# Stationary values in three kinds of attention, and one branch for an expert's gate and up products

## The chip, the cores and the metric

One kernel runs as one program on one core of a Trainium2 chip. The metric is the device time of one execution in microseconds (us), the median of several. Engines: TensorE (PE, matrix products; PEld is its weight load), VectorE (DVE), ScalarE (ACT), GpSimd (POOL) and SyncE (SP), which here issues the loads. Data lies in HBM, on chip in SBUF, and products land in PSUM.

## The reference

256 positions of width 1024 go through two blocks of two layers each, all in float32.

```python
# first block, layers i = 0 and 1: 16 query heads, 4 key/value heads, of 64
q, k, v = project_qkv(x, w_qkv[i], cos, sin)
a = moba_attention(q, k, v) if i == 0 else sliding_window_attention(q, k, v, sinks[0])
x = layer_norm(alpha * x + a @ w_o[i], ...)
f = swiglu(x, ...) if i == 0 else moe_swiglu(x, ...)
x = layer_norm(alpha * x + f, ...)
x = x + (p[i] @ w_ple_proj[i]) * sigmoid(x @ w_ple_gate[i])
...
# sliding window, with one sink per head
e = exp(logits - m)
probs = e / (sum(e) + exp(sink - m))
...
# eight experts, the best two of each position; expert: (silu(x Wg) * (x Wu)) Wd, width 3584
top_v, top_i = top_k(logits, 2)
# second block, both layers: gated delta rule (4 heads of 128) beside dilated attention
# (8 heads of 64, three dilations merged by their denominators), then a convolved GLU of 2816
```

With 256 positions the first layer's attention is plain causal attention, and one causal softmax with a table of weights does the three dilations.

## The kernel before

The Python code lists all operations of the network in program order. A planner (class Plan) then chooses, operation by operation, what each engine does next, by estimated costs and by how much work still hangs on an operation, and writes out one fixed order for each engine; a change in one place therefore reorders the neighbourhood. Nearly every instruction is issued by `call` (L756; copies by ACT at L754), so lines tell little, and tiles are known by tags: `raw` (5 slots of 512 KB for weights), `w4` (8), `v4` (4), `kv` (2), `mx` (15, in the experts only, where hi, lo and r4 give up their room by `layout(1)`), and in PSUM A (2), B (4) and C (2). Where the planner expects PE to idle, it may put in filler products (`identb`, 128x512, bf16).

Float32 weights outside the experts are split into a rounded part `hi` (ACT) and a rest `lo` (DVE or POOL), with three products each (A<-hi,r and so on).

Attention: `first_layer` calls `att_pair` for two parts (8 heads each) and two blocks b of 128 positions, four calls a layer; a dilated attention (in `mixer`) calls it for b = 0 and 1. With nk = b + 1 key blocks, scores of two groups of four heads land in PSUM C and B, DVE takes the row maximum, ACT the exponential (P). `att_out` then transposes P on PE, copies it out, multiplies it with V, which has a column of ones as its 65th so that the denominator comes out with the product (P as stationary operand, V moving, L1183), and DVE divides. `part_T` transposes the result (four 128x128) and splits it for the output projection w_o. Between the parts, `dense_tok` makes the query products of the next part, and the first half of w_o's contraction is done beside the second part.

Experts: `route` gives each position its slot among an expert's first 96. `fetch` loads the first 22 weight units (128x1024 float32) before the way into the experts. There, PE reads the eight counts into registers (L751), and all engines pass a branch over code for an expert with more than 96 rows (`overflow_experts`, L1634 and L294; jumped over with this input). Then, expert by expert, `expert_up` and `expert_out` go through four chunks of the width (1024, 1024, 1024, 512); a full chunk is 8 units of gate, 8 of up and 8 of down, 672 units in all. `tiled` multiplies slots 0 to 63 with each unit (stationary 64 columns, two halves of a unit side by side), and then, under a branch (L733) on the count over 64, slots 64 to 95 (stationary 32, four quarters side by side). A unit's slot comes free after both. With this input experts 1, 3, 6 and 7 take these branches. `raw_moe` is the rota by which units take their slots (28, of tags m = mx, r = raw, w = w4, v = v4, k = kv). `gather_pair` makes one-hot matrices of two experts on DVE and gathers their rows on PE.

Of the kernel before, what the change touches and what calls it, by code (L numbers as in the profile page):

```python
# [11 lines left out]
F32 = mybir.dt.float32  # L12
# [221 lines left out]
class Plan:  # L234
# [511 lines left out]
    def call(self, op, method, args, kw):  # L746
# [37 lines left out]
class Net:  # L784
    def __init__(self, ctx, tc, a, out):
# [8 lines left out]
        self.ahead = []  # L794
# [186 lines left out]
    def load(self, w, k0, nk, c0, n, tag=None):  # L981
# [4 lines left out]
        for h in range(2):  # L986
            raw = nc.tile([128, m, n], F32, "raw", *(tag or self.next_raw()))
            r0 = k0 + 128 * m * h
            nc.sync.dma_start(raw, lambda r0=r0: w[span(r0, 128 * m), span(c0, n)].rearrange("(t p) c -> p t c", p=128))
            raws.append(raw)  # L990
# [127 lines left out]
    def values(self, b, acc, n, va):  # L1118
        self.copy_out(va[:, b, :, 0:64], acc.rearrange("p (h d) -> p h d", d=64))

    def att_pair(self, kind, qT, kT, va, b, p, a):
# [6 lines left out]
        for g in (2 * p, 2 * p + 1):  # L1128
# [5 lines left out]
            groups.append((g, heads, self.ta([128, 4, nk, 128], "P"), self.sm([128, 4], "nm")))  # L1134
        for i0 in range(0, 4, per):
# [9 lines left out]
            with nc.group():  # L1145
                for i in range(per):
                    for kb in range(nk):
                        for ps, (_, heads, _, _) in zip(pss, groups):
# [5 lines left out]
            for ps, (g, heads, P, nm) in zip(pss, groups):  # L1154
# [9 lines left out]
    def att_out(self, kind, va, b, g, heads, P, nm, a):  # L1164
        nc = self.nc
        grouped = kind != "dilated"
        nk = b + 1
        per = 4 // nk
        PT = self.ta([128, 4, nk, 128], "PT")
        for i0 in range(0, 4, per):  # L1170
            ps = (self.pb if grouped else self.pa)([128, per, nk, 128], "PTp")
# [4 lines left out]
        po = (self.pb if grouped else self.pa)([128, 4, 65], "po")  # L1176
        for i in range(4):
            for kb in range(nk):
                nc.tensor.matmul(po[:, i, :], lhsT=PT[:, i, kb, :], rhs=va[:, kb, heads[i][3], :],
                                 start=kb == 0, stop=kb == nk - 1)  # L1180
        den = self.sm([128, 4, 1], "den")
        if kind == "swa":
            es = self.sm([128, 4], "es")  # L1183
            nc.vector.tensor_tensor(out=es, in0=nm, in1=self.nsink[:, 4 * g:4 * g + 4], op=OP.subtract)
            nc.scalar.activation(es, es, AF.Exp)
            nc.vector.tensor_tensor(out=den, in0=po[:, :, 64:65], in1=es[:, :, None], op=OP.add)
            nc.vector.reciprocal(den, den)
        else:
            nc.vector.reciprocal(den, po[:, :, 64:65])
        if grouped:  # L1190
            o = a[:, (g % 2) * 256:(g % 2) * 256 + 256].rearrange("p (h d) -> p h d", d=64)
        else:
            o = a.rearrange("p (i s d) -> p i s d", s=2, d=64)[:, :, g, :]
        nc.vector.tensor_tensor(out=o, in0=po[:, :, 0:64], in1=den.to_broadcast([128, 4, 64]), op=OP.mult)
# [233 lines left out]
    def gather_pair(self, e, xs, pos):  # L1428
# [736 lines left out]
```

## Time and profile before

| | us |
|---|---|
| median of 3 runs | 2221.87 |
| lowest and highest | 2221.15, 2225.56 |
| the profiled execution | 2224.77 |
| its span | 2223.0 |
| PE busy | 2102.1 |
| DVE, ACT, POOL busy | 984.3, 751.7, 224.7 |

Stages, in us from the span's start: first attention some 45 to 87, its output projection and norm to 125, FFN to about 390, second attention about 400 to 465, its output projection, norm and router to 492, experts to 1419, combine, norm and gate to 1478, the second block's layers to about 1850 and 2223, with dilated attention around 1600 to 1640 and 1960 to 2000.

How to read rows: a timeline row has the start, the length of a run of like instructions, engine, line, operation, what it writes from what, shapes and a count, and in brackets how long the engine idled before it and on whom. A matrix product's shape has the stationary operand's rows*columns first. Consecutive products overlap, so one that is counted costs the distance of starts. A stretches row has the stretch, its length, the busy time of PE, PEld, DVE, ACT and POOL (with counts), PE's granted clock, the mean busy share of 16 DMA engines, and GB/s. The trace has two records for each float32 product of the program.

### The profile page before, as it was taken

How to read it: one execution, taken by the hardware profiler on the slowest of the kernel's cores; microseconds unless marked ns; L12 is line 12 of the kernel's file. 1: busy time of each engine (PE TensorE's matmuls, PEld its weight loads, DVE VectorE, ACT ScalarE, POOL GpSimd, SP SyncE). 2: the span in 40 equal slices, each digit the busy share in tenths (PEclk: the TensorE clock that was granted, in tenths of full speed). 3: DMA queues.
4: the chain of work that ended last, by engine and by line, in shares of the span. 5: the costliest groups of instructions: out<-in, count | busy, mean ns of one | idle time of the engine just before them, and what ended most of it. 6: DMA issues, size and time to landing. Idle time of an engine off the chain costs nothing. (4 is left out here: it accounts for less than half of the span.)

```text
span 2223.0 us, 35510 instructions
## 1 busy us (share of the span) xinstructions
PE 2102.1 (95%) x14582; PEld 1449.2 (65%) x14582; DVE 984.3 (44%) x1670; ACT 751.7 (34%) x1141; POOL 224.7 (10%) x147
## 2 busy tenths in 40 slices
PE   8999999988799989998979999899999999999998
PEld 6899997763334323433233434479979997988997
DVE  6665467651010101010101001467687768768666
ACT  5544444420011101110110000356465556456554
POOL 0110001120000000000000000218020005411000
PEclk9999999989899999999999999999999999999999
DMA  7356664349999999999999998544455664435563
GB/s 251 111 165 192 184 184 152 114 159 345 404 388 370 373 404 409 385 372 404 408 404 394 369 396 326 188 145 144 130 170 183 190 183 141 124 97 187 175 194 117
DMA packets 246476, 557.48 MB, mean 251 GB/s; under 512 B 21320, under 2 KB 108552, under 8 KB 246280
## 3 DMA queue, kind: packets, MB, share of 16 engines
q1 hardware_dynamic: 246280, 554.72, 69.9%
q8 instruction: 141, 2.31, 0.4%
q14 instruction: 55, 0.45, 0.1%
HBM read 553.60 MB, written 1.05 MB: 250 GB/s over the span
## 5 line engine op out<-in xcount | busy, mean ns | idle before, releaser
L756 DVE TENSOR_TENSOR lo<-raw,hi 128x1024 fp32r<-128x1024 f32 x324 | 404.7, 1257 | 200.3 <-PE B L756 94.6
L756 ACT ACTIVATE hi<-raw 128x1024 fp32r<-128x1024 f32 x364 | 382.2, 1062 | 292.8 <-PE B L756 123.5
L756 PE MATMUL B<-r,hi 128*128 128x256 f32 x2112 | 388.2, 282 | 0.0
L756 PEld LDWEIGHTS B<-r,hi 128*128 128x128 f32 x2112 | 342.0, 191 | 17.7
L756 PE MATMUL B<-mx,w 128*64 128x512 f32 (+3 forms) x2188 | 327.9, 458 | 10.6 <-DMA mx<-in_w_exp_up_dram 8.4
L756 PE MATMUL A<-hi,r 128*128 128x512 f32 x896 | 334.3, 410 | 0.9 <-DVE v L756 0.6
L756 PE MATMUL B<-r,lo 128*128 128x256 f32 x1056 | 298.6, 283 | 0.0
L756 PEld LDWEIGHTS B<-mx,w 128*32 128x32 f32 (+1 forms) x2188 | 111.0, 124 | 153.1 <-issue 104.3
L756 PEld LDWEIGHTS B<-r,lo 128*128 128x128 f32 x1056 | 201.5, 191 | 0.0
L756 PEld LDWEIGHTS A<-hi,r 128*128 128x128 f32 x896 | 171.1, 191 | 32.2 <-DVE v L756 1.4
L756 PE MATMUL C<-hi,r 128*128 128x512 f32 x512 | 185.1, 400 | 1.1 <-ACT kv L756 1.1
L756 DVE MEMSET B<- 128x256 f32 (+1 forms) x64 | 15.7, 245 | 370.0 <-ACT w L756 366.6
L756 PE MATMUL A<-lo,r 128*128 128x512 f32 x448 | 177.4, 396 | 0.2 <-DVE lo L756 0.2
L756 PE MATMUL B<-w,w 128*128 128x128 f32 (+4 forms) x1252 | 168.4, 363 | 0.3 <-PEq L733 0.3
L756 PE MATMUL A<-mx,v 128*32 128x256 f32 (+1 forms) x960 | 162.1, 491 | 0.2 <-PEq L733 0.2
L754 ACT ACTIVATE v<-C 128x512 f32<-128x512 f32 (+2 forms) x63 | 29.4, 467 | 379.8 <-PE C L756 336.0
L756 DVE TENSOR_TENSOR w<-w,B 128x256 f32<-128x256 f32 (+2 forms) x79 | 41.8, 529 | 247.9 <-PE B L756 229.7
L756 POOL TENSOR_TENSOR lo<-raw,hi 128x1024 fp32r<-128x1024 f32 x40 | 102.0, 2563 | 487.8 <-ACT hi L756 367.4
L756 PEld LDWEIGHTS B<-w,w 128*128 128x128 f32 (+2 forms) x1252 | 104.5, 155 | 51.4 <-issue 39.6
L756 ACT ACTIVATE w<-B 128x256 f32<-128x256 f32 (+3 forms) x95 | 44.7, 475 | 264.8 <-PE B L756 242.9
L756 PEld LDWEIGHTS C<-hi,r 128*128 128x128 f32 x512 | 98.5, 192 | 18.8 <-ACT kv L756 1.9
L756 PE MATMUL B<-raw,w 128*64 128x512 f32 (+3 forms) x648 | 100.9, 463 | 1.3 <-DMA raw<-in_w_exp_up_dram 1.0
(239 smaller groups left out, 2602.1 us busy)
## 6 DMA issues: line engine op xcount, KB each, us to landing
mx<-in_w_exp_up_dram SPq DMA_DIRECT2D x124, 512.0 KB, 10.2
mx<-in_w_exp_down_dram SPq DMA_DIRECT2D x120, 512.0 KB, 10.3
mx<-in_w_exp_gate_dram SPq DMA_DIRECT2D x119, 512.0 KB, 8.0
raw<-in_ffn_up_dram SPq DMA_DIRECT2D x88, 512.0 KB, 3.7
raw<-in_w_in_dram SPq DMA_DIRECT2D x56, 512.0 KB, 3.8
raw<-in_w_exp_down_dram SPq DMA_DIRECT2D x48, 512.0 KB, 10.2
w<-in_w_exp_up_dram SPq DMA_DIRECT2D x46, 512.0 KB, 10.2
raw<-in_ffn_down_dram SPq DMA_DIRECT2D x44, 512.0 KB, 4.5
```

Source lines behind the costliest of these rows:

```text
L754: eng.activation(args[0], args[1], AF.Copy)
L756: getattr(eng, method)(*args, **kw)
```

## The change

- `att_pair` now sums each exponential (`accum_out`), adds the sink's term in the sliding window, takes the reciprocal and multiplies P by it, before P is transposed (`heads_last`). `att_values` multiplies with V stationary (64 columns, no ones) and the transposed P moving, two groups side by side, so that the result comes out already transposed and goes straight to the split. `att_out` and `part_T` behind it are gone.
- w_o is loaded by heads (`by_heads`), each load as two of 64 partitions.
- `fetch` takes 28 units; the first 7 (raw and kv slots) before `layout(1)`. The steady rota has 24 slots: no v, no k.
- `tiled` takes gate and up together: both 64-slot passes, then one branch with both 32-slot passes.
- `values_load` is made without its bounds check. The first pair's one-hots are made ahead of the overflow branch.

```diff
-            kw["to"].cell[0] = self.nc.values_load(args[0], engines=[mybir.EngineType.PE], min_val=0, max_val=S)
+            kw["to"].cell[0] = self.nc.values_load(args[0], engines=[mybir.EngineType.PE],
+                                                       skip_runtime_bounds_check_because="it is the sum of 256 zeros and ones")
...
-        self.raw_first = [("raw", RAW)] * RAW + [("kv", 2)] * 2 + [("mx", 15)] * 15
-        size = {"m": ("mx", 15), "r": ("raw", RAW), "w": ("w4", 8), "v": ("v4", 4), "k": ("kv", 2)}
-        self.raw_moe = [size[c] for c in "mrmwmrmvmwmkmrmwmrmvmwmkmrmm"]
+        self.raw_first = [("raw", RAW)] * RAW + [("kv", 2)] * 2 + [("mx", 15)] * 15 + [("w4", 8)] * 4 + [("v4", 4)] * 2
+        size = {"m": ("mx", 15), "r": ("raw", RAW), "w": ("w4", 8)}
+        self.raw_moe = [size[c] for c in "mrmwmmrmwmmrmwmmrmwmmrmm"]
...
+            if self.by_heads:
+
+                for s in range(2):
+                    r0 = k0 + 256 * s + 64 * m * h
+                    nc.sync.dma_start(raw[64 * s:64 * s + 64], w[r0:r0 + 64 * m, c0:c0 + n].rearrange("(t p) c -> p t c", p=64))
...
-        va = self.nc.tile([128, 2, HK, 65], F32, "va", "kv", 2)
-        self.nc.gpsimd.memset(va, 1.0)
+        va = self.nc.tile([128, 2, HK, 64], F32, "va", "kv", 2)
...
-                for i in range(per):
-                    nc.scalar.activation(P[:, i0 + i], ps[:, i], AF.Exp, bias=nm[:, i0 + i:i0 + i + 1])
-        for g, heads, P, nm in groups:
-            self.att_out(kind, va, b, g, heads, P, nm, a)
...
+                hs = slice(i0, i0 + per)
+                for i in range(i0, i0 + per):
+                    nc.scalar.activation(P[:, i], ps[:, i - i0], AF.Exp, bias=nm[:, i:i + 1], accum_out=den[:, i])
+                if kind == "swa":
+                    es = self.sm([128, per, 1], "es")
+                    nc.vector.tensor_tensor(out=es[:, :, 0], in0=ns, in1=self.nsink[:, 4 * g + i0:4 * g + i0 + per], op=OP.subtract)
+                    nc.scalar.activation(es, es, AF.Exp)
+                    nc.vector.tensor_tensor(out=den[:, hs], in0=den[:, hs], in1=es, op=OP.add)
+                nc.vector.reciprocal(den[:, hs], den[:, hs])
+                part = P[:, hs].rearrange("p i k j -> p i (k j)")
+                nc.vector.tensor_tensor(out=part, in0=part, in1=den[:, hs].to_broadcast([128, per, nk * 128]), op=OP.mult)
+        self.att_values(kind, va, b, [(heads, P) for _, heads, P, _, _ in groups], [t[k] for t in aT.tiles])
...
+        PT = [self.heads_last(P, nk, pool) for _, P in groups]
+        po = pool([128, 4, 128], "po")
+        with nc.group():
+            for i in range(1 if grouped else 4):
+                hs = slice(None) if grouped else i
+                for kb in range(nk):
+                    for s, (heads, _) in enumerate(groups):
+                        nc.tensor.matmul(po[64 * s:64 * s + 64, hs], lhsT=va[:, kb, heads[i][3], :], rhs=PT[s][:, hs, kb, :],
+                                         start=kb == 0, stop=kb == nk - 1)
+        self.split_ps(po, *[t[:, :, b * 128:b * 128 + 128] for t in dst])
...
+        for acc, tiles in sums:
+            for k, u in enumerate(tiles):
+                n = u.shape[1]
+                with nc.group():
+                    for i in range(2):
+                        mm(acc[0][64 * i:64 * i + 64, :n // 2], lhsT=slots(k, 0, 64), rhs=u[:, i * n // 2:(i + 1) * n // 2],
+                           start=first and k == 0, stop=last and k == len(tiles) - 1)
         with nc.group((count, 64, 1.0)):
-            for k, u in enumerate(tiles):
-                for i in range(4):
-                    mm(acc[1][32 * i:32 * i + 32, :n // 4], lhsT=slots(k, 64, 32), rhs=u[:, i * n // 4:(i + 1) * n // 4],
-                       start=whole and k == 0, stop=whole and k == k1 - 1)
+            for acc, tiles in sums:
+                for k, u in enumerate(tiles):
+                    n = u.shape[1]
+                    for i in range(4):
+                        mm(acc[1][32 * i:32 * i + 32, :n // 4], lhsT=slots(k, 64, 32), rhs=u[:, i * n // 4:(i + 1) * n // 4],
+                           start=whole and k == 0, stop=whole and k == len(tiles) - 1)
...
+        P = self.pair_one_hots(0, pos)
         self.overflow_experts(logits, rank, xs, pos)
...
         else:
+            self.fetch(RAW + 2)
             nc.layout(1)
             self.moe(logits)
```

PE in the first attention, last call (part 1, b = 1), before (ident marks a transpose, kv with v the product of P and V, A<-hi or lo w_o's products over part 0):

```order
L756 MATMUL B3_139<-ident0_91,v20_153 128x128 x2
L756 MATMUL B2_138<-ident0_91,v41_141 128x128 x4
L756 MATMUL B1_137<-kv0_144,v40_140 128x65 x4
L756 MATMUL B0_136<-ident0_91,v43_143 128x128 x2
L756 MATMUL B1_137<-kv0_144,v40_140 128x65 x4
L756 MATMUL B0_136<-ident0_91,v43_143 128x128 x2
L756 MATMUL A0_146<-hi0_1_72,r44_1_68 128x512
L756 MATMUL A0_146<-lo2_1_80,r44_1_68 128x512
L756 MATMUL A0_146<-hi0_1_72,r45_1_69 128x512
L756 MATMUL B2_138<-kv0_144,v42_142 128x65 x8
```

and after (v with kv: V stationary in kv, P moving in v; identb alone: filler):

```order
L757 MATMUL B0_136<-ident0_91,v42_142 128x128 x2
L757 MATMUL B3_139<-ident0_91,v41_141 128x128 x4
L757 LDWEIGHTS identb0_92
L757 MATMUL C0_157<-identb0_92 128x512
L757 LDWEIGHTS identb0_92
L757 MATMUL C0_157<-identb0_92 128x512
L757 MATMUL B2_138<-v40_140,kv1_145 64x512
L757 MATMUL B2_138<-v43_143,kv1_145 64x512
L757 MATMUL B2_138<-v40_140,kv1_145 64x512
L757 MATMUL B2_138<-v43_143,kv1_145 64x512
```

The products of 65 columns among the transposes have become four of 64 stationary and 512 moving columns, in one group behind all transposes, and two fillers stand before them.

PE ahead of the overflow branch, before (count: a register load; ISA: its check instructions; the two rows with count repeat eight times):

```order
L756 LDWEIGHTS before0_102
L756 MATMUL B1_137<-sm12_119,before0_102 128x8
L756 LDWEIGHTS onesb0_103
L756 MATMUL B0_136<-sm12_119,onesb0_103 128x8
L751 TENSOR_LOAD count0_189
L751 ISA x2
```

and after:

```order
L757 LDWEIGHTS onesb0_103
L757 MATMUL B3_139<-sm15_122,onesb0_103 128x8
L757 LDWEIGHTS identb0_92
L751 TENSOR_LOAD count0_189 x8
L757 MATMUL A1_147<-identb0_92 128x512
L757 LDWEIGHTS identb0_92
```

The eight loads now follow one another with nothing between them.

DVE at the overflow branch, before (most: the largest count; L294: the branch):

```order
L756 SCALAR_TENSOR_TENSOR pos_187<-B_137,sm_121 128x16
L756 TENSOR_REDUCE sm_124<-B_136 128x1
L756 CAST count_189<-B_136 128x8
L756 CAST most_188<-sm_124 128x1
L1634 TENSOR_LOAD most_188
L294 COMPARE_AND_BRANCH
L756 TENSOR_SCALAR sm_123<-sa_181 128x16
```

and after (iota, pos: one-hots, r_169):

```order
L757 SCALAR_TENSOR_TENSOR pos_187<-B_138,sm_128 128x16
L757 CAST count_189<-B_139 128x8
L757 TENSOR_REDUCE sm_125<-B_139 128x1
L757 TENSOR_SCALAR r_169<-iota_106,pos_187 128x128
L757 CAST most_188<-sm_125 128x1
L757 TENSOR_SCALAR r_169<-iota_106,pos_187 128x128 x3
L1657 TENSOR_LOAD most_188
L294 COMPARE_AND_BRANCH
```

The first pair's one-hots, which stood behind the branch, now stand before it.

PE at a branch of a first chunk, before (mx, raw, w, v or kv: unit; 64x512 and 32x256: products of slots 0 to 63 and 64 to 95; B: PSUM):

```order
L756 MATMUL C_157<-ident_91,w_88 128x128 x4
L733 COMPARE_AND_BRANCH
L756 MATMUL B_136<-w_159,w_162 32x256 x4
L756 MATMUL B_136<-mx_2_4000,w_162 32x256 x4
L756 MATMUL B_136<-raw_150,w_162 32x256 x4
L756 MATMUL B_136<-mx_2_3992,w_162 32x256 x4
L756 MATMUL B_136<-v_140,w_164 32x256 x4
L756 MATMUL B_136<-mx_2_3997,w_164 32x256 x4
L756 MATMUL B_136<-w_160,w_164 32x256 x4
L756 MATMUL B_136<-mx_2_3990,w_164 32x256 x4
L733 UNCONDITIONAL_BRANCH x2
L756 MATMUL C_157<-r_169,r_193 128x512
```

and after (at an expert's first branch, its first 12 of 18 rows):

```order
L733 COMPARE_AND_BRANCH
L757 MATMUL B_136<-raw_148,w_165 32x256 x4
L757 MATMUL B_136<-raw_152,w_165 32x256 x4
L757 MATMUL B_136<-raw_149,w_165 32x256 x4
L757 MATMUL B_136<-raw_150,w_165 32x256 x4
L757 MATMUL B_136<-raw_151,w_166 32x256 x4
L757 MATMUL B_136<-kv_144,w_166 32x256 x4
L757 MATMUL B_136<-kv_145,w_166 32x256 x4
L757 MATMUL B_136<-mx_2_3942,w_166 32x256 x4
L757 MATMUL B_137<-mx_2_3939,w_165 32x256 x4
L757 MATMUL B_137<-mx_2_3940,w_165 32x256 x4
L757 MATMUL B_137<-mx_2_3945,w_165 32x256 x4
```

One branch now covers the 32-slot products of sixteen units, gate into B_136 and up into B_137, where it covered eight.

## Rows read from the trace of the kernel before

**Rows 1.** Page, the chain that ended last, share of the span by engine:

```profile
PE 41%; DVE 3%; issue 1%; ACT 0%; POOL 0%; DMA 0%; DVEq 0%; POOLq 0%; SPq 0%; ACTq 0%
```

**Rows 2.** Stretches table: stretch, its length, engines' busy time, clock, DMA share, GB/s:

```profile
45.00:87.00 42.00, 42.00 (x337) 36.18 (x334) 26.73 (x56) 25.24 (x54) 0.53 (x1) 1.00 0.23 78
...
400.00:465.00 65.00, 61.80 (x426) 51.54 (x425) 42.81 (x105) 33.42 (x72) 7.56 (x3) 1.00 0.20 68
...
512.00:1166.00 654.00, 593.24 (x3935) 231.41 (x3933) 71.43 (x179) 62.70 (x129) 6.24 (x12) 0.96 1.00 391
...
1166.00:1419.00 253.00, 252.52 (x2319) 105.65 (x2315) 24.08 (x56) 20.04 (x43) 2.01 (x3) 0.99 0.92 356
...
1600.00:1640.00 40.00, 38.30 (x260) 32.50 (x258) 34.75 (x48) 29.03 (x50) 13.08 (x9) 1.00 0.54 174
...
1960.00:2000.00 40.00, 39.02 (x266) 33.13 (x265) 25.80 (x36) 22.77 (x38) 7.59 (x5) 1.00 0.33 103
```

**Rows 3.** Timeline of PE in the first attention (start, us, engine, operation):

```profile
79.50 0.82 PE L756 MATMUL B<-ident,v 128*128 128x128 f32 x6
...
83.04 1.89 PE L756 MATMUL B<-kv,v 128*128 128x65 f32 x16
```

**Rows 4.** Instructions by form, PE, whole span: count, busy us, mean ns, idle before:

```profile
L756 PE MATMUL B<-kv,v 128*128 128x65 f32 x192 | 24.8, 268 | 0.0
...
L756 PE MATMUL A<-kv,v 128*128 128x65 f32 x96 | 12.9, 276 | 0.6 <-ACT v L754 0.6
```

**Rows 5.** Timeline of PE in experts 6 and 7:

```profile
1204.43 1.06 PE L756 MATMUL B<-raw,w 128*64 128x512 f32 x4
...
1205.29 1.06 PE L756 MATMUL B<-mx,w 128*64 128x512 f32 x4
...
1243.61 1.03 PE L756 MATMUL B<-w,w 128*64 128x512 f32 x4
1244.57 0.64 PE L756 MATMUL A<-kv,v 128*32 128x256 f32 x8
1245.03 0.61 PE L756 MATMUL A<-mx,v 128*32 128x256 f32 x8
```

**Rows 6.** Instructions by form, DVE and ACT, whole span:

```profile
L756 DVE TENSOR_TENSOR w<-w,w 128x512 f32<-128x512 f32 x30 | 24.5, 815 | 7.7 <-ACT w L756 5.2 <-DVE w L756 0.5
...
L756 DVE TENSOR_TENSOR v<-B,sm 128x256 f32<-128x256 f32 x16 | 6.8, 422 | 0.4
...
L756 ACT ACTIVATION_READ_ACCUMULATOR w<-x 128x1 f32 x16 | 3.0, 187 | 0.0
```

**Rows 7.** Around the overflow branch: PE's sequencer (L751, L294), then DVE and PE:

```profile
L751 PEldq TENSOR_LOAD <-count x8: 297/303/497, 492.0 to 497.2; - x8
...
L294 PEldq COMPARE_BRANCH  x1: 6055/6055/6055, 498.4 to 498.4; - x1
...
504.65 1.41 DVE L756 TENSOR_SCALAR r<-iota,pos 128x128 fp32r<-128x128 f32 x4 [12.57 <-PEq L294]
...
497.86 5.09 PE L756 MATMUL A<-identb 128*128 128x512 bf16 x15 [6.31 <-issue]
...
506.13 3.59 PE L756 MATMUL C<-r,xs 128*128 128x256 f32 x24 [3.19 <-DVE sm L756]
```

**Rows 8.** Stretches of 10 us in the experts:

```profile
734.00:744.00 10.00, 9.51 (x53) 3.08 (x53) 1.01 (x3) 1.15 (x3) 0.00 (x0) 1.00 0.57 204
...
814.00:824.00 10.00, 5.04 (x32) 2.07 (x29) 1.15 (x4) 0.24 (x2) 0.00 (x0) 0.91 1.03 408
...
1154.00:1164.00 10.00, 0.46 (x5) 0.22 (x3) 0.42 (x1) 0.60 (x1) 0.52 (x1) 0.63 1.03 410
```

**Rows 9.** Timeline of SP's DMA issues behind the overflow branch:

```profile
514.77 0.46 SPq L756 DMA_DIRECT2D w<-in_w_exp_down_dram  x1
...
524.16 0.33 SPq L756 DMA_DIRECT2D raw<-in_w_exp_gate_dram  x1
```

**Rows 10.** Line L733, the experts' branches, on PE's sequencer (min/median/max ns):

```profile
L733 PEldq COMPARE_BRANCH  x144: 65/176/632, 519.6 to 1416.2; - x144
```

More of the change, by code (lines that the diff above doesn't have):

```diff
@@ L1170, in att_out @@
         for i0 in range(0, 4, per):
-            ps = (self.pb if grouped else self.pa)([128, per, nk, 128], "PTp")
+            ps = pool([128, per, nk, 128], "PTp")
             for i in range(per):
@@ L1175, in att_out, with att_values @@
             self.copy_out(PT[:, i0:i0 + per], ps)
-        po = (self.pb if grouped else self.pa)([128, 4, 65], "po")
-        for i in range(4):
[L1178 to L1194, printed above, removed]
+        return PT
+    def att_values(self, kind, va, b, groups, dst):
+        nc = self.nc
+        nk = b + 1
+        grouped = kind != "dilated"
+        pool = self.pb if grouped else self.pa
+        PT = [self.heads_last(P, nk, pool) for _, P in groups]
[8 more added lines that the diff above has]
+        self.split_ps(po, *[t[:, :, b * 128:b * 128 + 128] for t in dst])
     def ple_proj(self, i):
@@ L1457, in weights, with fetch @@
         return raw
-    def fetch(self):
+    def fetch(self, n):
         self.raw_tags = self.raw_first
-        for name, c0, n in (("gate", 0, 8), ("up", 0, 8), ("gate", 1024, 6)):
-            for k in range(n):
-                key = "w_exp_" + name, 0, 128 * k, c0
-                self.raws = len(self.fetched) - 1
-                self.fetched[key] = self.weights(*key[:3], 1, c0, 1024)
-    def tiled(self, acc, slots, units, count, first, last):
+        keys = [("w_exp_" + name, 0, 128 * k, c0) for c0 in (0, 1024) for name in ("gate", "up") for k in range(KT)]
+        for i in range(len(self.fetched), n):
+            key = keys[i]
+            self.raws = i - 1
+            self.fetched[key] = self.weights(*key[:3], 1, key[3], 1024)
+        self.raw_tags = [("raw", RAW)]
@@ L1471, in tiled @@
+    def tiled(self, sums, slots, count, first, last):
         nc = self.nc
         mm = nc.tensor.matmul
-        tiles = [u[:, t, :] for u in units for t in range(u.shape[1])]
-        n = tiles[0].shape[1]
-        k1, whole = len(tiles), first and last
-        for k, u in enumerate(tiles):
-            with nc.group():
-                for i in range(2):
-                    mm(acc[0][64 * i:64 * i + 64, :n // 2], lhsT=slots(k, 0, 64), rhs=u[:, i * n // 2:(i + 1) * n // 2],
-                       start=first and k == 0, stop=last and k == k1 - 1)
@@ L1481, in tiled @@
-        with nc.group((count, 64, 1.0)):
-            for k, u in enumerate(tiles):
-                for i in range(4):
-                    mm(acc[1][32 * i:32 * i + 32, :n // 4], lhsT=slots(k, 64, 32), rhs=u[:, i * n // 4:(i + 1) * n // 4],
-                       start=whole and k == 0, stop=whole and k == k1 - 1)
+        sums = [(acc, [u[:, t, :] for u in units for t in range(u.shape[1])]) for acc, units in sums]
+        whole = first and last
+        for acc, tiles in sums:
[5 more added lines that the diff above has]
+                           start=first and k == 0, stop=last and k == len(tiles) - 1)
@@ L1494, in expert_up @@
             nc.vector.memset(acc[1][:, :n // 4], 0.0)
-            units = [self.weights(w, e, 128 * k, nk, c0, n) for k in range(0, KT, nk)]
-            j = 128 * (e % 2)
-            self.tiled(acc, lambda k, s, m: xg[k // 4][:, k % 4, j + s:j + s + m], units, count, True, True)
-            ps.append(acc)
+            sums.append((acc, [self.weights(w, e, 128 * k, nk, c0, n) for k in range(0, KT, nk)]))
+        self.tiled(sums, lambda k, s, m: xg[k // 4][:, k % 4, j + s:j + s + m], count, True, True)
+        ps = [acc for acc, _ in sums]
         hT = self.ta([128, 6, 128], "hT")
@@ L1519, in slots @@
             return hT[:, 4 + f, 32 * i:32 * i + 32]
-        self.tiled(y, slots, units, count, first, last)
+        self.tiled([(y, units)], slots, count, first, last)
     def zero(self, acc, start):
@@ L1593, in moe @@
         nc, a, tc = self.nc, self.a, self.tc
-        self.fetch()
+        self.fetch(len(self.raw_first))
         rank, pos = self.route(logits)
```

48 lines of the change are left out of this document (25 added, 23 removed).

## The prediction

> **What bounds the kernel now.** I read the page's chain first, then the stretches table, then the rows of four places that the change touches. TensorE (PE) carries the chain of work that ended last [rows 1]. The reader is to see in [rows 2] three kinds of stretch. In the first attention (45 to 87 us) PE is busy for all 42.00 us: what leaves PE there leaves the span, so long as nothing else is late. In the second (400 to 465) and the dilated ones (1600 to 1640, 1960 to 2000) PE idles 1.0 to 3.2 us. In the experts from 512 to 1166 the DMA share is 1.00 and PE idles 61 us: loads set the pace. From 1166 to 1419, under experts 6 and 7, PE is busy again for all but 0.5 us. So three prices apply: PE time counts in attention and in the last experts; between them only what lets loads start earlier, or stops them, counts.
>
> **Attention.** The values products of before are 192 + 96 records of 65 moving columns [rows 4]; sixteen take 1.89 us [rows 3], less the 0.27 us that the last one overhangs 0.108 us each. The trace writes each float32 product as two records, the order as one. Per first-block layer that is 96 x 0.108 = 10.4 us; 16 transposes of the head outputs, at (0.82 - 0.27) / 5 = 0.11 us [rows 3], go as well: 1.8 us. In their place stand 24 records with 64 stationary and 512 moving columns. An expert's product of that form takes four records in 0.86 us (1204.43 to 1205.29, [rows 5]), 0.215 each: 5.2 us. PE saves 7.0 us a layer.
>
> For a dilated attention 48 records go (5.2 us) with 8 transposes (0.9), and 48 with 64 stationary and 128 moving columns come. No row shows that form. Bounds are 0.108 us, if each is held as the old ones were, and 0.054, a quarter of the 512-column row. The nearest row is the expert's 32-slot product, also with few columns a record: eight in 0.46 us (1244.57 to 1245.03, [rows 5]), 0.058. I take that: 2.8 us, so 3.3 us saved a layer; at the upper bound 0.9.
> The 65-column rows have just been seen to cost half of a 512-column record for an eighth of its columns. The Trainium skill, TensorEngine Tiling (Array Packing), Performance Considerations, gives up to a factor of two for such a swap of stationary and streaming operand when 64 columns are stationary, but warns against taking the factor from a dimension that is already small. By its factor the dilated products would cost 2.6 us, by its warning up to the old 5.2; the row of the 32-slot product speaks for the first.
>
> Against PE's saving stands a longer softmax. P is now scaled before it is transposed: 36 DVE products of 128x512 (12 in each first-block layer, 6 in each dilated one) at 0.815 us, the nearest row from SBUF to SBUF [rows 6], 29 us; 24 output products of 0.42 us go [rows 6], 10 us. Each of 96 exponentials now also sums its row. The trace shows such a sum as a record of its own, 0.187 us [rows 6]: 18 us of ACT, 6.0 in a first-block layer; at least nothing, if it overlapped. One call's chain thus grows by up to 8 x 0.187 = 1.5 us on ACT and 0.8 to 1.6 us on DVE. In 45 to 87 DVE and ACT are busy 26.7 and 25.2 us [rows 2]. With 12 x 0.815 - 8 x 0.42 = 6.4 more, DVE would have 33.1, ACT 31.2, of 35 us that the full saving leaves. That is tight, and the order there has 11 filler products against 4, each 5.09 / 15 = 0.34 us [rows 7]: 2.4 us of PE that the planner could not fill. I take 4 of 7.0 us. In 400 to 465 DVE has 42.8 of 65 us: I take 5. Of the dilated 3.3 I take 2.5 each. Together **-14 us**; bounds 0, if the longer chain eats all, and 2 x 7.0 + 2 x 3.3 = 20.6.
>
> The output weights now come as two half-partition loads each, 16 more issues a layer; no row shows such a load. DMA share there is 0.20 to 0.23 [rows 2], so I count nothing. Without that cover eight loads at most doubled would cost 8 x 1.28 = 10 us (0.524 MB at the 410 GB/s of [rows 8]). The V memset on POOL leaves: nothing, POOL is nearly idle there.
>
> **The way into the experts.** PE reads eight counts from 492.0 to 497.2 [rows 7], one each 0.74 us, of which the load is 0.30; the rest are the check instructions that go. 8 x 0.44 = 3.5 us earlier it reaches the branch over the overflow code, which takes 6.06 us [rows 7]. Then DVE, idle for 12.57 us behind the same branch, makes the first pair's one-hots at 504.65 and PE's gather starts at 506.13 [rows 7]. Those one-hots now stand before DVE's branch: 1.5 us more. Together **-5 us**. These reach the experts' end only if the loads shift too. Before, 22 units are fetched before the branch and 8 behind it (the last at 514.77), then SP waits for PE's first released slot at 524.16 [rows 9]; after, 28 and 2. Either way 30 units stand ready at PE's first release, which comes 5 us earlier, so the saturated stretch starts earlier by as much. The seven fetches that now start before the layout switch and fill an idle DMA buy nothing beyond this: the pool is full either way.
>
> **Branches and slots.** Gate and up share one branch: 96 become 64, and the changes between 64-slot and 32-slot products in experts 6 and 7, counted in the order, fall from 108 to 81. Such a change costs 0.96 - 0.86 = 0.10 us (1243.61 to 1244.57, [rows 5]): **-2.7 us**, all on PE's path [rows 2]. In the earlier experts this hides under the loads.
> The steady pool falls from 28 to 24 slots and the 16 slots of a chunk's gate and up are held until their common branch. Where a heavy expert (over 64 rows: 1, 3, 6, 7) makes PE slow, slots are full and loads pause: DMA share 0.57 in 734 to 744 [rows 8]. After it PE lives on that lead until it starves, 5.04 of 10 us busy in 814 to 824 and 0.46 in 1154 to 1164 [rows 8]. Four slots less are 4 x 1.28 = 5.1 us less lead at each of the two passages from a heavy to a light expert (1 to 2, 3 to 4): 0 if the lead was never whole, 10.2 if it always was. I take the middle, **+5**.
>
> **Sum.** -14 - 5 - 2.7 + 5 = -16.7 us. The profiled execution, its span of 2223.0 us and 1.8 us around it, took 2224.8 us and would take 2208.1. It lies 2.9 us above the median of the runs shown, 2221.9; on that footing the forecast is **2205 us**.
>
> **Rivals.**
> (A) *The softmax chain becomes the bound*, and the attentions gain 0 to 2 us. For it: the two engines' tight sums in 45 to 87. Against it: PE has the next part's query products, and w_o's first half, to do meanwhile. Time: 2221.9 - 5 - 2.7 + 5 - 1 = 2218.
> (B) *All PE time counts*: -20.6 - 5 - 2.7 = -28.3, 2194 us. For it: 42.00 of 42.00. Against it: the fillers, the shorter lead.
> (C) *Slower, too few slots*: while PE does sixteen 64-slot units (16 x 0.86 = 13.8 us) only 8 of 24 slots take loads, 10.2 us, so loads rest 3.6 us in each of some 7 full chunks of experts 1 and 3, 25 us, besides the 10 us of lead. 2221.9 - 14 - 5 - 2.7 + 35 = 2235. It decides once loads lose over 26 us more before 1166 than before. For it: loads already rest there [rows 8]. Against it: the branch frees its sixteen slots one by one, and in light experts PE waits for loads, so slots are free.
> (D) *The change doesn't do what it says at the branch*: the gather waits for something else (SP's part of the barrier, the jump itself), and the 5 us stay: 2210.
> (E) *Longer jumps cost more.* A skipped expert branch now jumps over twice the instructions. So far branches take 0.065 to 0.632 us [rows 10], the jump over the overflow code 6.06 [rows 7]. If the 16 gate-and-up jumps in light experts each cost that, 97 us, less the 61 us that PE waits anyway, make +36: 2241 from the forecast. Against it: no branch of 144 took over 0.632.
> The Trainium skill, Runtime: NRT & Kernel Launch, Instruction fetch mechanics, says that a taken branch whose target lies outside the prefetched window stalls for a fetch. The 6.06 us agree with such a stall; the branches of now show none.
>
> **How the numbers follow.** Chances: forecast 0.53 (2198 to 2214), A 0.13, B 0.13, C 0.08, D 0.10, E 0.03. The range 2192 to 2224 takes in A, most of B and D, and leaves out C, E and the edge of B, 0.16. A measurement of this kernel tells about 0.2%, 4.4 us, from no change. Faster by more: the forecast, B, D and a part of A, 0.77; within: most of A, 0.12; slower: C and E, 0.11.
>
> **What would show it.** Right: PE in the first attention has 7 us less products, its stretch ends 3 to 6 us earlier; values records of 64x512 at 0.215 us; the first gather 9 us, not 14.1, behind the first read of a count; experts 6 and 7 take 250 us against 253. Wrong: PE idle in the attentions behind DVE's scaling or ACT's sums (A); DMA share under 0.9 in more windows before the last starved one (C); expert branches over 1 us (E); the gather still 14.1 us behind the first read of a count (D).

## The result

The changed kernel takes 2192.3 us (median of four, 2190.0 to 2193.3), the kernel before 2221.5 beside it: ratio 0.9863, 95% interval [0.9851, 0.9875], some 30 us less. The forecast was 2205 with a range from 2192 to 2224; the ratio puts the time at 2191.4 on the forecast's own base, just under the range, and near rival B (2194), though not for B's reason.

The profiled execution of after has a span of 2190.0 us against 2223.0. Since such spans wander by some 3 us, I read both kernels twice: once from the profiles at hand, once from two executions side by side on another chip (before_again, after_again below). The times are starts in the trace, from the span's start:

| event, us | before | again | after | again |
|---|---|---|---|---|
| first read of a count | 492.0 | 490.7 | 483.5 | 482.9 |
| PE's first gather | 506.1 | 504.4 | 493.8 | 493.2 |
| last branch of an expert | 1416.2 | 1413.8 | 1391.0 | 1393.9 |
| end of the span | 2223.0 | 2219.8 | 2190.0 | 2193.4 |

Subtracting neighbouring lines gives what each stretch gained, and beside it what the prediction had:

| stretch | gained (two pairs) | predicted |
|---|---|---|
| first block up to the router | 8.5, 7.8 | 9 |
| counts, branch, first gather | 3.8, 3.4 | 5 |
| experts, gather to last branch | 12.9, 8.7 | -2.3 (2.7 - 5) |
| from there to the end, with two dilated attentions | 7.8, 6.5 | 5 |

Three of the four stretches came out about as worked out. The experts did not: they were to lose 2 us and gained 9 to 13. First the rows of the three, since they answer [rows 1 to 3, 6 and 7]; what experts 6 and 7 gained [rows 5] stands at the end of the experiments.

The chain that ended last, page of after (share of the span by engine), reads as [rows 1] did; PE still carries it:

```profile
PE 42%; DVE 2%; issue 1%; POOL 1%; ACT 1%; DMA 0%; DVEq 0%; POOLq 0%; ACTq 0%; SPq 0%
```

The stretches table of after (length, busy us of PE, PEld, DVE, ACT, POOL, granted clock, DMA share, GB/s), answering [rows 2]:

```profile
45.00:87.00 42.00, 40.52 (x255) 27.61 (x254) 34.24 (x62) 27.91 (x84) 7.23 (x3) 1.00 0.35 90
...
400.00:456.00 56.00, 52.24 (x316) 36.60 (x314) 47.03 (x113) 35.21 (x104) 7.66 (x3) 1.00 0.41 104
...
512.00:1150.00 638.00, 585.97 (x3902) 227.70 (x3900) 65.33 (x166) 66.25 (x140) 6.23 (x12) 0.97 1.00 396
```

In 45 to 87 PE now idles 1.5 us where it idled none, and DVE is busy for 34.2 us instead of 26.7 (the same 42 us hold a little more of the next stage by now): the longer softmax shows, as forecast, but does not take the gain back. In the experts the DMA share is 1.00 as before, and the clock 0.97 against 0.96; yet the rate in the last column is 396 GB/s over a stretch that held 391.

PE's values products in the first attention, timeline of after, answering [rows 3]; and the last run of them in the first dilated attention with the product behind it:

```profile
75.74 1.08 PE L757 MATMUL B<-v,kv 128*64 128x512 f32 x4
...
82.03 1.99 PE L757 MATMUL B<-v,kv 128*64 128x512 f32 x8 [0.19 <-DVE v L757]
```

```profile
1607.41 1.97 PE L757 MATMUL A<-v,kv 128*64 128x128 f32 x32
1609.31 0.50 PE L757 MATMUL C<-hi,r 128*128 128x512 f32 x1
```

Four records with 64 stationary and 512 moving columns give way to the next product 1.0 us after they start (76.75), 0.25 each; 32 of the dilated ones take 1609.31 - 1607.41 = 1.90 us, 0.059 each. The prediction took 0.215 and 0.058. Before, sixteen of the old form took 1.89 us.

The scaling of P on DVE, and the row sum of an exponential on ACT, by form over the whole span (count, busy us, mean ns, idle before), answering [rows 6]:

```profile
L757 DVE TENSOR_TENSOR v<-v,sm 128x512 f32<-128x512 f32 x36 | 30.6, 859 | 0.5
```

```profile
L757 ACT ACTIVATION_READ_ACCUMULATOR v<-B,sm 128x1 f32 x48 | 10.6, 222 | 0.0
```

0.859 us a product against 0.815 assumed; the row sums 0.222 (0.210 for the 48 out of PSUM C) against 0.187.

At the branch, lines L751 and L294 on PE's sequencer, then DVE's one-hots and PE's gather in the timelines of after, answering [rows 7]:

```profile
L751 PEldq TENSOR_LOAD <-count x8: 296/308/496, 483.5 to 486.5; - x8
```

```profile
L294 PEldq COMPARE_BRANCH  x1: 6112/6112/6112, 487.4 to 487.4; - x1
```

```profile
483.88 0.66 DVE L757 TENSOR_SCALAR r<-iota,pos 128x128 fp32r<-128x128 f32 x3
```

```profile
493.79 3.13 PE L757 MATMUL C<-r,xs 128*128 128x256 f32 x24 [2.52 <-PEq L294]
```

From the first to the last of eight counts it is 3.0 us where it was 5.2; the jump takes 6.1 us as before; three of the four one-hots stand at 483.88, ahead of the branch (the first at 483.41), and PE gathers as soon as the jump lets it, 10.3 us behind the first read (14.1 before).

### The profile page after: what moved, and what is told of

The parts are those of the page before. It is cut to its first block, busy times and chain, and to the rows that moved or that the text cites. A ratio compares the mean times of both kernels' runs of the same rounds, so it can differ in the third digit from the quotient of the medians.

```text
span 2190.0 us, 35283 instructions
## 1 busy us (share of the span) xinstructions
PE 2076.3 (95%) x14383; PEld 1416.5 (65%) x14383; DVE 983.7 (45%) x1671; ACT 770.1 (35%) x1263; POOL 243.5 (11%) x152
## 5 line engine op out<-in xcount | busy, mean ns | idle before, releaser
L757 DVE TENSOR_TENSOR lo<-raw,hi 128x1024 fp32r<-128x1024 f32 x315 | 392.3, 1253 | 190.7 <-PE B L757 95.7
L757 PE MATMUL B<-mx,w 128*64 128x512 f32 (+3 forms) x2428 | 349.0, 458 | 25.8 <-DMA mx<-in_w_exp_up_dram 12.0
L757 PEld LDWEIGHTS B<-mx,w 128*64 128x64 f32 (+1 forms) x2428 | 123.1, 124 | 193.7 <-issue 122.1
L757 PE MATMUL A<-mx,v 128*32 128x256 f32 (+1 forms) x1208 | 193.7, 491 | 7.5 <-DMA mx<-in_w_exp_down_dram 3.9
L757 POOL TENSOR_TENSOR lo<-raw,hi 128x1024 fp32r<-128x1024 f32 x49 | 125.9, 2582 | 644.7 <-ACT hi L757 574.7
L757 PE MATMUL B<-w,w 128*128 128x128 f32 (+4 forms) x1328 | 183.8, 371 | 0.8 <-PEq L733 0.8
L755 ACT ACTIVATE v<-C 128x512 f32<-128x512 f32 (+2 forms) x56 | 26.7, 477 | 391.4 <-PE C L757 391.3
L757 DVE TENSOR_TENSOR w<-w,B 128x256 f32<-128x256 f32 (+1 forms) x79 | 41.8, 530 | 269.7 <-PE B L757 167.6
L757 ACT ACTIVATE w<-B 128x256 f32<-128x256 f32 (+2 forms) x95 | 44.7, 476 | 317.5 <-PE B L757 272.3
L757 PE MATMUL B<-raw,w 128*64 128x512 f32 (+3 forms) x884 | 133.4, 456 | 9.5 <-DMA raw<-in_w_exp_gate_dram 5.3
L757 PEld LDWEIGHTS A<-mx,v 128*32 128x32 f32 (+1 forms) x1208 | 58.6, 124 | 99.4 <-issue 76.0
```

What stands on the lines that cost most here:

```text
L755: eng.activation(args[0], args[1], AF.Copy)
L757: getattr(eng, method)(*args, **kw)
```

## Experiments

### Is the gain in the experts the kernel's, or the chip's?

In stretches of 10 us with a DMA share of 1.02 or more, from 510 to 1150 us, the profile of before moves 408 GB/s (median of 54 stretches), that of after 417 (50). Two profiles from two chips might differ so by chance, so both ran again side by side, and each kernel with the other's rota of slots. before_again and after_again change nothing.

> The kernel before, unchanged, profiled beside the three runs that follow. In the two profiles at hand the saturated stretches of the experts moved 408 to 411 GB/s before and 415 to 420 after. Theory R (the rate comes with the change): here 408 to 411 again, and the experts take as long as before, 506 to 1419 us in the trace. Theory S (the rate belongs to the execution or the chip, not to the kernel): here the same rate as in the run of the changed kernel beside it, and if that is 415 or more, experts some 13 us shorter than in the first profile of before.

> The changed kernel, unchanged, profiled beside the others. Theory R: 415 to 420 GB/s in saturated 20 us stretches, against 408 to 411 in the run of before beside it. Theory S: the same rate in both, whatever it is.

One stretch of 20 us in the experts, kernel before and then the changed one, on one chip (last column GB/s):

```profile
820.00:840.00 20.00, 15.42 (x60) 5.19 (x60) 0.00 (x0) 0.52 (x1) 0.00 (x0) 0.75 1.03 410
```

```profile
820.00:840.00 20.00, 17.97 (x124) 6.45 (x124) 1.23 (x3) 1.78 (x3) 0.00 (x0) 0.91 1.03 418
```

408 and 418 as medians over the saturated stretches: the rate belongs to the kernel.

The rota in the changed kernel, back to 28 slots:

```diff
-        self.raw_moe = [size[c] for c in "mrmwmmrmwmmrmwmmrmwmmrmm"]
+        self.raw_moe = [size[c] for c in "mrmwmrmvmwmkmrmwmrmvmwmkmrmm"]
```

> The changed kernel with the steady rota of before: 28 slots with four of tag v and two of tag k in it, instead of 24 of m, r and w. If the rota gives the rate or ends waits for loads into v and k slots (theory R): 2192 + 12 to 16 = 2204 to 2208 us, 409 GB/s, and PE waits of some 10 us on loads into v slots again. If the 24 slots only cost lead, as the prediction had it (+5): 2187. If the rota is worth nothing: 2192 within 3.

2204.9 us, ratio 0.991 [0.9892, 0.9928], 10 to 13 us slower than after, but at 417 GB/s. So the rota is worth something here, and not through the rate: PE's longest waits for loads now fall on raw units (waits of PE: total, times, longest).

```profile
PE B L757 <- DMA raw<-in_w_exp_gate_dram: 25.1, 5, 8.5
...
PE B L757 <- DMA raw<-in_w_exp_up_dram: 20.2, 5, 6.5
```

> The kernel before with the steady rota of the changed one alone (24 slots, no v, no k). Theory R: 2221.5 - 12 to 16 = 2206 to 2210 us, 418 GB/s. The prediction's term: 2221.5 + 5 = 2226 (at most +10). Worth nothing: 2221 within 3.

The same rota alone on the kernel before: 2224.8, ratio 1.001 [1.0000, 1.0021], +2 us, 408 GB/s. Theory R in the form "the rota gives the rate" falls. The prediction's +5 for four slots less is just above the interval's upper end (4.7), and by the profile the loss is not where the prediction had it: from gather to last branch this kernel takes 904.0 us, 6 less than before (910.1 and 909.4), and from there to the end 811.4, 5 more (806.8 and 806.0). Behind the last branch the planner's order differs (5295 records of PE products against 5288).

### Places in SBUF

What else differs in the experts? The instructions of a load are the same. Their addresses are not. V lost its 65th column, V of a dilated attention was the largest tile of tag kv, and so the two kv slots shrank from 4160 to 4096 bytes a partition. All tiles allocated behind them moved: raw and w4 by 128 bytes, and the mx slots too, from 128 past a multiple of 256 bytes to a multiple of 256 (addresses of the compiled programs). Four kernels with the same instructions in the same order move them alone.

```diff
+            if tag == "kv":
+                n = 1040        # after_kv1040; 1152 in before_kv1152
             info["aps"] = [pools[info["space"]].tile([128, n], F32, ...
```

> The changed kernel, same instructions in the same order, but the two kv slots are 4160 bytes a partition again, as before (V with its 65th column had made them so), in place of 4096; every tile allocated behind them moves by 64 and 128 bytes. Theory P (places in SBUF set the load rate): 408 to 411 GB/s in saturated stretches instead of 414 to 419, and 2193 + 8 to 16 = 2201 to 2209 us. Theory N (the rate comes with the new order of branches or loads): 414 to 419 GB/s, 2193 within 3.

```profile
820.00:840.00 20.00, 18.03 (x77) 4.97 (x73) 0.27 (x1) 1.32 (x3) 0.00 (x0) 0.96 1.03 409
```

The same stretch in the changed kernel with the old kv slots: 409 GB/s, and 2201.6 us.

> The kernel before, same instructions in the same order, with kv slots of 4608 bytes a partition (a multiple of 512) in place of 4160. Theory P: 414 to 419 GB/s and 2222 - 8 to 16 = 2206 to 2214 us. Theory N: 408 to 411 GB/s and 2222 within 3.

```profile
820.00:840.00 20.00, 19.63 (x130) 7.17 (x130) 0.27 (x1) 1.26 (x3) 0.00 (x0) 0.91 1.03 419
```

The kernel before with kv slots of 4608 bytes: 419 GB/s and 2210.9 us, ratio 0.996 [0.9938, 0.9981], -9 us. Theory P holds both ways, with every instruction in its old place.

That pad moved raw, w4 and mx together. Two more move the mx slots without raw and w4, by an unused tile of 128 bytes behind the small ones (the gathered rows xs lie in front of mx and move with it):

```diff
+        pools[SB].tile([128, 32], F32, name="pad1", tag="pad1")
```

> The changed kernel, same instructions, with 128 unused bytes behind the small tiles: mx slots start 384 past a multiple of 512 as before (128 past one of 256), raw, kv, v4 and w4 stay where the change has them. If mx's start sets the load rate: 409 GB/s and 2201 us, as with the old kv slots. If raw's and w4's does: 418 GB/s and 2192. If both share it: 412 to 415 and 2196 or so.

```profile
820.00:840.00 20.00, 19.11 (x73) 5.73 (x75) 0.27 (x1) 0.88 (x2) 0.00 (x0) 0.84 1.03 409
```

> The kernel before, same instructions, with the same 128 unused bytes: mx slots start at a multiple of 512, raw and w4 stay 352 past one. If mx's start sets the rate: 415 to 419 GB/s in stretches that load mostly mx, and 2221 - 6 to 11 = 2210 to 2215 us (only 15 of its 28 slots are mx, so a part of the rate may be left). If raw's and w4's does: 409 and 2221.

```profile
820.00:840.00 20.00, 17.72 (x116) 6.77 (x120) 0.27 (x1) 0.60 (x1) 0.00 (x0) 0.86 1.03 420
```

2202.7 us for the changed kernel with mx at its old remainder, 2215.1 (0.9968 [0.9956, 0.9980], -7 us) for the kernel before with mx at a multiple of 256. So the start of the mx slots is enough to make the rate. Over all twenty profiles there are just two rates: 408 in the nine with mx at byte 166272, 417 to 418 in the eleven with mx at another start, always a multiple of 256; attention, branches, rota and prefetch do not move it. The single DMA packets show the same: between 512 and 1150 us 95 to 98% of those of 4096 bytes take 159 or 160 ns in the eleven, but 46 to 53% in the nine, where nearly all others take 161 to 180. Which of them go into mx slots the traces do not say.

Would a rounder start give more? after_512 puts all weight slots at multiples of 512 by two such unused tiles. It ran twice, the second time (after_512_5) beside the changed kernel (after_5).

```diff
+            if tag == "v4":
+                pools[SB].tile([128, 72], F32, name="pad0", tag="pad0")
...
+        pools[SB].tile([128, 120], F32, name="pad1", tag="pad1")
```

> The changed kernel, same instructions in the same order, with two unused tiles put in so that all weight slots (raw, kv, w4, v4, mx) start at multiples of 512 bytes; in the changed kernel mx starts 256, raw, kv, v4 and w4 224 past such a multiple, in the kernel before mx 384, raw and w4 352. Theory P in the form 'the rounder the start, the faster the loads': over 419 GB/s in saturated stretches and 2193 - 3 to 12 = 2181 to 2190 us. If only mx at a multiple of 256 counts: 2193 within 3 and 414 to 419.

> The changed kernel, timed beside the next one: 2190 to 2195 us, 414 to 419 GB/s.

> The changed kernel with all weight slots at multiples of 512 bytes, timed beside the last one. If 512 is worth more than 256: 3 to 6 us faster than it. If not: within 2 us of it, at the same 414 to 419 GB/s.

```profile
820.00:840.00 20.00, 18.43 (x164) 6.79 (x164) 1.23 (x3) 2.17 (x4) 0.00 (x0) 1.00 1.03 419
```

The rate stays at 417 to 418. Yet the time is 2187.7 and 2187.6 us, against 2194.9 for the changed kernel in the same call (ratios to before 0.9850 [0.9835, 0.9866] and 0.9886 [0.9868, 0.9903]). This version beats both. Where its 7 us lie is open: its experts take 898.1 us from gather to last branch against 899.7, and the other stretches differ by less than two executions of one kernel do.

### The parts alone, and taken out

> The kernel before with the attention part of the change alone (scaled P, stationary V, no transposes of the result, half-partition loads of w_o), kv slots kept at 4160 bytes. The prediction's term: -14 us, 2208 (9 us until the first read of a count, 5 in the dilated ones). Its rival A: 2220 or more. Its rival B: 2201. No change of the load rate by either theory on it, 409 GB/s.

The attention part on the kernel before (its diff is the attention part of the change, with kv slots kept at 4160): 2210.5 us, 0.9953 [0.9939, 0.9967], -10.4 us. Its experts take 909.7 us, as before (910.1, 909.4).

> The changed kernel without its attention part, mx slots at a multiple of 512. If attention gives what it gave alone: 2193 + 10 = 2203 to 2205. If part of its 10 us was lost again under the saturated loads of the experts: 2196 to 2200. If it gives more in company: over 2207.

The changed kernel without it, mx at a multiple of 512: 2204.2 us, so attention is worth 9 to 12 us there as well, by the medians. No loss of it under the loads shows.

> The kernel before with the reads of the counts unchecked and the first pair's one-hots ahead of the overflow branch, nothing else. The prediction's term: -5 us, the first gather 9 us behind the first read of a count in place of 14.1, and 2222 - 5 = 2217. Its rival D: gather at 14 us and 2222. If the earlier start is given back under the saturated loads: gather at 9 to 10 us and 2220 to 2222.

Reads and one-hots alone: 2216.6 us, 0.9980 [0.9967, 0.9993], -4.4 us. PE's reads of the counts, and its gather, in this kernel:

```profile
L751 PEldq TENSOR_LOAD <-count x8: 297/306/497, 490.7 to 493.8; - x8
```

```profile
501.04 4.42 PE L757 MATMUL C<-r,xs 128*128 128x256 f32 x24 [1.81 <-PEq L294]
```

501.0 - 490.7 = 10.3 us, as in the changed kernel. Rival D is out.

> The kernel before with gate and up under one branch alone, with its rota of 28 slots and kv slots of 4160 bytes. The prediction: -2.7 us for fewer changes of product, a loss up to 5 for slots held longer: 2219 to 2227. Theory N: 414 to 419 GB/s and 2206 to 2214. Theory P: 409 GB/s.

The common branch alone:

```diff
-            self.tiled(acc, ..., units, count, True, True)      # one call for gate, one for up
+        self.tiled(sums, ..., count, True, True)                # both sums, one branch
```

2228.8 us, 1.0041 [1.0028, 1.0054]: +9 us. Its branches, and PE's wait for the loads into v slots (total, times, longest), here and, second, in the kernel before:

```profile
L733 PEldq COMPARE_BRANCH  x96: 65/176/6085, 521.6 to 1413.1; - x96
```

```profile
PE B L756 <- DMA v<-in_w_exp_gate_dram: 24.4, 7, 6.6
...
PE B L756 <- DMA v<-in_w_exp_gate_dram: 34.9, 4, 11.1
```

That wait has become shorter, so it is not what the 9 us are. The profile has its experts at 907.2 us from gather to last branch, 2 to 3 less than before, and 811.2 behind them, 5 more; the order there differs as in before_rota24 (5295 records again).

> The kernel before with the common branch and the 24-slot rota, nothing else; kv slots of 4160 bytes. Alone the branch cost 9 us (2229) and the rota 2 (2225). If they add: 2222 + 11 = 2233. If the rota of large pools mends what the common branch costs, as the changed kernel with the old rota (10 to 12 us slower than with the new) suggests: 2219 to 2223.

With the new rota beside it: 2224.1, 1.0010 [0.9999, 1.0021], +2 us. The two do not add. But this kernel's experts take 912.8 us, and behind them it is 806.6 as before: the +2 hides a loss of 3 in the experts, near the 2.3 that were forecast, though not by its terms (below).

> The changed kernel with gate and up under their own branches again (96 branches), all else as changed. If the common branch costs what it cost alone (+9 us in the run before these): 2193 - 9 = 2184. If it pays by fewer changes of product (the prediction's -2.7): 2196. If the common branch and the 24-slot rota only make sense together: 2193 to 2200.

The changed kernel with two branches: 2199.4, 0.9909 [0.9889, 0.9929], 4 to 7 us slower than with one by the medians. In the changed kernel the common branch pays, or does no harm. Its experts take 900.3 us, between 897.2 and 900.7, so most of the difference lies elsewhere.

> The changed kernel with the prefetch of before (22 units, none ahead of the layout switch), mx slots as in the changed one. The prediction counted the longer prefetch as nothing: 2192 to 2196 us. If it carries what is left of the sum: 2196 to 2200. If eight loads behind the branch serve as well or better: 2188 to 2192.

The changed kernel with the old prefetch: 2198.1, 0.9884 [0.9866, 0.9902]; the changed kernel's own intervals (0.9863 and 0.9886) overlap it. Inconclusive between 0 and 6 us.

### The experts, split in two

Since these parts also reorder what stands around them, their stretches say more than their times. The table splits the experts at the last branch of expert 5: loads bound the first stretch, PE the second. The last column is PE's waits put down to the expert branches.

| kernel | GB/s | first gather to there | experts 6, 7 | last branch to end | waits on branches |
|---|---|---|---|---|---|
| before, again | 408 | 746.5, 745.7 | 163.6, 163.7 | 806.8, 806.0 | 8.2, 7.3 |
| before_rota24 | 408 | 740.2 | 163.8 | 811.4 | 7.7 |
| branch_only | 408 | 747.3 | 159.9 | 811.2 | 10.7 |
| branch_rota24 | 408 | 753.5 | 159.3 | 806.6 | 20.5 |
| before_mx256 | 417 | 739.4 | 163.6 | 807.4 | 7.9 |
| after, again | 417, 418 | 738.7, 742.2 | 158.5, 158.5 | 799.0, 799.5 | 7.0, 7.8 |
| after_mx128 | 408 | 749.2 | 158.5 | 800.3 | 5.4 |
| all_but_branch | 418 | 736.5 | 163.8 | 801.9 | 7.8 |
| after_rota28 | 417 | 748.3 | 159.3 | 801.0 | 10.7 |

The two rows of experts 6 and 7, before and after (the first branch is expert 5's last):

```profile
L733 PEldq COMPARE_BRANCH  x37: 65/169/179, 1252.6 to 1416.2; - x37
...
L733 PEldq COMPARE_BRANCH  x25: 65/169/179, 1232.5 to 1391.0; - x25
```

mx at a multiple of 256 is worth 6 to 7 us in the first stretch of the kernel before, 7 to 11 in the changed one. The common branch saves 4 to 5 us in experts 6 and 7 in every kernel that has it. The new rota saves 6 us in the first stretch alone, 6 to 10 in the changed kernel, but costs 6 in branch_rota24, where long jumps (below) hold PE for 20.5 us.

## Why the prediction was wrong

**The missing term.** The sum held a price for every instruction that goes, comes or moves, and none for where the tiles lie. The step "the steady pool falls from 28 to 24 slots: +5" was about the right question, what the loads can do in the experts, but asked only how many may be in flight and not how fast each is. Its sign failed too: the 24-slot rota made the first stretch of the experts 6 us shorter alone, and 6 to 10 in the changed kernel. The changed V shape stood in the diff (65 to 64 columns), and the prediction booked it as a memset less on POOL, "nothing". It was worth 7 to 10 us: -7 and -9 on the kernel before, +7 to +10 when taken back from the changed one (2201.6 and 2202.7 against 2192.3 and 2194.9). At 408 GB/s a unit of 0.524 MB takes 1.285 us, at 417.5 it takes 1.256; over the 672 units that would be 20 us, were every load on the path. PE sets the pace in parts, so a third to a half arrives.

The Trainium skill, DMA: Bandwidth & Descriptors, How a descriptor splits into AXI transactions, says that a descriptor is cut at multiples of 256 bytes, and that a piece which starts off one still pays for the bytes from the boundary below; whether that holds for the SBUF side of a load it does not say. Worked out from it, a row of 4096 bytes that starts 128 past a boundary takes 132 beats of 32 bytes instead of 128, 3.1% by this estimate. Measured are 2.3%, but over the loads of all slots, and only 363 of 672 units go into mx before (417 after): were only these longer, the estimate would make 1.7 to 1.9%. By the same reading the raw and w4 slots, 96 or 224 past a boundary, should cost too, and the runs show nothing of that: 417 to 418 GB/s with them there and with them at multiples of 512. So the remainder of mx is shown to set the rate, and how it does so is open.

**Attention: right, its size a little large.** -14 predicted; alone -10.4 [-13.6, -7.3], and in the pairs of profiles 8 up to the router and 6.5 to 7.8 behind the experts, most of which is dilated attention's (5.3 to 6.1 with attention alone: 806.0 to 806.8 from last branch to end before, 800.7 in att_only_kv1040). The dilated form (no row before) costs what its nearest row said, 0.059 us against 0.058, the one of 512 columns 0.25 against 0.215. The first block's 9 us were split 4 and 5 between the layers; at the first layer's norm (DVE's BATCH_NORM_AGGREGATE at 103.8 and 101.7 us before, 98.1 and 97.1 after) the gain was already 5.7 and 4.6, and some 3 came later: the sum fits better than its parts. DVE's load in the first attention rose to 34.2 us against the 33.1 worked out, and PE idled 1.5 us. The half-partition loads of w_o are 16 more in all, not in each layer (32 where there were 16), and no engine waits for one. Rival A is out, and rival B's full 20.6 us too.

**The way into the experts: right, 1 us too large.** The reads take 0.43 us each, (486.5 - 483.5) / 7, not the 0.30 of a single load: 8 x (0.74 - 0.43) = 2.5 us instead of 3.5. With 1.5 for the one-hots that makes 4.0; 3.4 to 3.8 measured in the profiles, 4.4 [1.6, 7.3] in time.

**Branch and slots: a size and a sign.** With the old address the changed kernel's experts take 908.3 us (after_kv1040) and 907.7 (after_mx128) against 910.1 and 909.4: 2 us less, where 2.3 more were forecast. The common branch was priced at -2.7 in experts 6 and 7 and gave -5.1 there (158.5 against 163.6); alone -3.7. The rota was priced at +5 and gave -6 alone. Where both stand with the old address, the first stretch takes 749 to 754 us and not the rota's 740, so they do not add.

**Rival C** did not come: from 510 to 1150 the stretches of 10 us with a DMA share under 0.9 are seven before and six after. **Rival E** came in its sign, long expert branches, but not for its reason, and in the changed kernel at no price that shows. The expert branches on PE's sequencer, after, answering [rows 10]:

```profile
L733 PEldq COMPARE_BRANCH  x96: 65/176/5765, 507.7 to 1391.0; - x96
```

Four jumps take 1.2, 2.1, 3.0 and 5.8 us, 12 us in all, where the longest was 0.63 before. Twice the code under a jump is not what makes them: with the old, short branches the longest took 2.2 us in entry_only, 3.3 in before_rota24, 3.7 in all_but_branch and 4.0 in att_only_kv1040. And PE's waits put down to the branches (total, times, longest) are no more than before, 7.0 us against 8.2 (after, then before):

```profile
PE A L757 <- PEq L733: 3.7, 7, 2.6
...
PE B L757 <- PEq L733: 2.3, 10, 0.9
...
PE C L757 <- PEq L733: 1.0, 6, 0.2
...
PE C L756 <- PEq L733: 3.6, 15, 0.4
...
PE B L756 <- PEq L733: 2.9, 16, 0.4
...
PE A L756 <- PEq L733: 1.7, 7, 0.4
```

That is not so in every kernel: in branch_rota24 five jumps take 22.5 us together, PE waits 20.5 us on branches, and its experts are the longest of all. What the long jumps wait for, the traces show. In the longest of after (745.21 to 750.97 us) lies one packet of the instruction queue (q8); it ends at 749.6. Such packets, of 16384 bytes, come every 12 us or so in the experts (73 from 519 to 1417 us in before). All 59 expert branches over 1 us in the twenty profiles end 1.37 to 1.53 us after the end of one of them: they wait for code. The Trainium skill, Runtime: NRT & Kernel Launch, Instruction fetch mechanics, says that a taken branch whose target is not in the prefetched window forces a fetch of the target's page, and the traces agree. Why the packet comes in time in the kernel before, and late in others, is open.

**What stays open.** Parts alone: attention -10.4, entry -4.4, mx's start -7 to -9, branch with rota +2, together -20 to -22; the whole is -25 to -30 (its two ratios). The 3 to 10 us between are of the size of the intervals; the longer prefetch, counted as nothing, may hold up to 6 of them (all_but_fetch), and the +2 of branch with rota holds 12 us more of waits on branches than before, which the changed kernel does not have. The runs don't settle the shares.

## To carry to other kernels

A change of a tile's shape is also a change of the address of everything allocated behind it: list the starts of the tiles that carry the loads before and after, and price the loads at both remainders. Where loads are the bound, look at the rate within saturated stretches (here 408 and 417 GB/s at the same busy share of 1.03), since the busy share stays the same while the bytes behind it change. A part of a change timed alone also reorders what it does not touch, so read it by stretches and not by its time (the common branch alone: +9 us in all, yet 3.7 less in experts 6 and 7, where it acts, and 5 more in the last layer).

## What the hardware showed that was not expected

- With the 15 mx slots at a start 128 bytes past a multiple of 256 the saturated loads (units of 0.524 MB) run at 408 GB/s, at a multiple of 256 at 417 to 418, in every kernel tried; 512 instead of 256 changes nothing in the rate. The lower rate was seen at one start (byte 166272), the higher at four, so the rule "256" is the simplest that fits, not a proven one. Slots of other tags at 96 or 224 past showed no loss.
- A branch of 0.07 to 0.2 us takes 1 to 6.5 us a few times in a run (6.5 in after_again, 6.1 in branch_only, 3.7 in all_but_branch, none over 0.63 before), all seen between 520 and 1150 us, in which loads mostly saturate. Each of these 59 ends 1.37 to 1.53 us after a 16384-byte packet of the instruction queue has landed.
- Reads of a count into PE's register follow one another every 0.43 us, though each lasts 0.30.
